# Where a split weight begins in SBUF: moving the up-product weights of a float32 decoder trunk by 32 bytes

## The chip, the cores and the metric

The kernel runs on one core of a Trainium2 chip. A core has a matrix engine (TensorE; PE in the profile, its weight loads PEld), a vector engine (DVE), an activation engine (ACT), GpSimd (POOL) and a queue engine (SP) that issues transfers. All of them work on one on-chip memory, SBUF, which has 128 partitions; a tile is the same range of bytes in every partition. Products are written to a second memory, PSUM. The metric is the device time of one execution in microseconds (us), the median of three runs.

## The reference

The reference is a trunk of four residual blocks on 512 tokens with a model width of 1024, all in float32: multi-head latent attention, a multi-layer perceptron (MLP), gated linear attention, and a second MLP, with an RMS norm ahead of each and one at the end. The MLP is where most of the arithmetic lies:

```python
def sq_relu_mlp(xn, w_up, w_down):            # w_up 1024 x 4096, w_down 4096 x 1024
    hid = jnp.square(jax.nn.relu(xn @ w_up))
    return hid @ w_down
...
x = x + sq_relu_mlp(rms_norm(x, norm_mlp[i]), mlp_w_up[i], mlp_w_down[i])
```

## The kernel before, in words

**Split products.** The matrix engine is used in a float32 mode (`float32r`) that keeps only part of the mantissa, so each operand is split into a high part and the rest. ACT rounds the source into the high part (L104), DVE subtracts to get the low part (L107), and a product is three matrix multiplications: high times high, high times low, low times high. The split weights are called `wh` and `wl`. `piece` (L137) makes such a pair; each of the two tags has three buffers, which all weights of the program use in turn.

A matrix multiplication has a stationary operand, which a weight load (LDWEIGHTS) brings into the array, and a moving operand, which streams through it. Every multiplication here has a weight load of its own, and the load for the next one runs while the current one streams.

**The MLP.** `mlp` runs each layer as a first block of hidden columns (`up_first`, L846) and then seven steps (`step`, L951), one for each further block of 512 hidden columns. Within a step both the up and the down product are cut into quadrants and done with seven quadrant products in place of eight (Strassen's scheme in Winograd's form). So a step has seven up products (`up_product`, L931) and seven down products (`down_product`, L941), which alternate on the matrix engine:

- An up product takes 512 x 256 weights. It has 24 multiplications of 128 x 128 stationary weights (slices of `wh` and `wl`) with 256 moving columns (L939). The moving operand is a split quadrant of the normed activations. Three of the seven quadrants ("11", "21", "22") are halves of tiles of the norm, made by `both_parts` (L96) and called `set` in the profile; the other four are sums of quadrants in tiles of their own, `T1` to `T4` (`quadrants`, L864; the profile calls them all T).
- A down product takes 256 x 512 weights. It has 12 multiplications with 512 moving columns (L948); here the split weights are the moving operand and the split hidden activations, also called `set`, are stationary.

Two layers of seven steps make 14 steps. The weights of the next block come in while a block is computed (`fetch`, L913): SP issues the plain transfers into `comb` and `wraw`, and POOL issues transfers that add to what SP's brought (L918 and L928, four in a step). POOL's transfers are written as lists of descriptors into a scratch region at the bottom of SBUF, 16,384 bytes of each partition.

**What sets the order.** The kernel is written in a tile language with a scheduler: the order of the work follows the order in which the code allocates and issues, with the buffers' reuse as the bound. Tiles get their addresses from the pools, in the order in which their tags first appear. In both programs the order of the instructions on all five engines is the same, row for row; only addresses and line numbers differ. (Two weight tiles, `w_kr` and `wa`, go by the names `wh` and `wl` afterwards.)

**Where the tiles lie.** Start of an operand in its partition, as a remainder of 512 bytes (slices within a tile begin at multiples of 512 bytes, so the remainder is the same for all slices of one tile):

| operand | used as | before | after |
|---|---|---|---|
| `wh`, `wl` in up products | stationary | 32 | 0 |
| `wh`, `wl` everywhere else | stationary or moving | 32 | 32 |
| `set` (norm quadrants, hidden activations, attention outputs) | both | 32 | 32 |
| `T1` to `T4` | moving | 320 | 288 |
| `comb`, two of six buffers (made after the T tiles) | source of splits | 320 | 288 |
| `comb`, the other four | source of splits | 320 | 320 |
| `cq`, the split query latents of attention | moving | 128 | 128 |
| `ckv`, its split key and value latents | moving | 192 | 192 |
| `ADh`, `ADl` in the linear attention (L1515) | stationary | 320 | 320 |

"Distance" below is the moving operand's remainder less the stationary operand's, again as a remainder of 512.

Of the kernel before, what the change touches and what calls it, by code (L numbers as in the profile page):

```python
# [10 lines left out]
F32 = mybir.dt.float32  # L11
F32R = mybir.dt.float32r
# [6 lines left out]
P = 128  # L19
# [3 lines left out]
ND = D // P  # L23
# [5 lines left out]
ROPE = 64  # L29
# [6 lines left out]
RANK = 16  # L36
# [14 lines left out]
def trunk_kernel(ctx: ExitStack, tc: tile.TileContext, t_in: dict, out: bass.AP):  # L51
    nc = tc.nc
# [3 lines left out]
    sb = ctx.enter_context(tc.tile_pool(name="sb", bufs=1))  # L56
    count = [0]

    def uname(s):
        count[0] += 1  # L60
        return f"{s}_{count[0]}"
# [14 lines left out]
    def bank(tag):  # L76
        return psum["pool"].tile([P, 512], F32, tag=f"ps_{tag}", bufs=psum["banks"][tag], name=uname("ps"))
# [11 lines left out]
    def tmp(shape=(P, 512), dt=F32):  # L89
        return sb.tile(list(shape), dt, tag="tmp", bufs=6, name=uname("tmp"))  # L90
# [11 lines left out]
    def split(src, hi, lo, hi_eng=ACT, lo_eng=DVE, order=lambda i: i):  # L102
        if hi_eng is ACT:
            order(ACT.activation(hi, src, AF.Copy))  # L104
        else:
            hi_eng.tensor_copy(hi, src)
        lo_eng.tensor_tensor(lo, src, f(hi), ALU.subtract)  # L107
# [26 lines left out]
        SP.dma_start(raw, src)  # L134
        return raw

    def piece(raw, a, n, order=lambda i: i):  # L137
        hi = sb.tile([P, a, n], F32R, tag="wh", bufs=3, name=uname("wh"))
        lo = sb.tile([P, a, n], F32R, tag="wl", bufs=3, name=uname("wl"))
        split(raw, hi, lo, order=order)  # L140
        return hi, lo

    def cut(pair, *idx):
        return tuple(t[idx] for t in pair)
# [56 lines left out]
    def gcol(name, j):  # L201
        c = GAIN_COL[name] + j
        return gains[:, c : c + 1]
# [166 lines left out]
    def col_chunk(w2d, c0, n):  # L370
        return load(w2d[:, c0 : c0 + n].rearrange("(k p) n -> p k n", p=P), w2d.shape[0] // P, n)


    def mla(layer, nrm, first, pools):
# [36 lines left out]
        KH = ND // 2  # L411
        raw = sb.tile([P, ND, 256], F32, tag="wraw", bufs=2, name=uname("wraw"))
        wq = []
        for h in range(2):
            ks = slice(h * KH, (h + 1) * KH)
            SP.dma_start(raw[:, ks], w_in[:, :256].rearrange("(k p) n -> p k n", p=P)[:, ks])
            wq.append(piece(raw[:, ks], KH, 256))
        for j in range(2):
            p = bank("c")
# [10 lines left out]

        raw = col_chunk(w_in, 256, P)
        w = piece(raw, ND, P)
        p = bank("b")
        a_type(p, w, X)
# [2 lines left out]


        raw = col_chunk(w_in, QL + KL, ROPE)
        wr = sb.tile([P, ND, 2, ROPE], F32R, tag="wh", bufs=3, name="w_kr")  # L440
        ACT.activation(wr[:, :, 1, :], raw, AF.Copy)
        DVE.tensor_tensor(wr[:, :, 0, :], raw, f(wr[:, :, 1, :]), ALU.subtract)
        p = bank("b")
# [23 lines left out]
        raw = sb.tile([P, 2, MH, VD], F32, tag="wraw", bufs=2, name="wraw_v")  # L467
        for k in range(2):
            SP.dma_start(raw[:, k], w_ukv[:, k, :, NOPE:])
        wv = [piece(raw[:, k : k + 1].rearrange("p a h c -> p a (h c)"), 1, D) for k in range(2)]  # L470
        V = [[None, None] for _ in range(NT)]
        VP = []
# [13 lines left out]
        for t in range(NT):  # L486
            tk = slice(t * P, (t + 1) * P)
            for hf in range(2):
                p = bank("bc"[hf])
# [15 lines left out]
            if t == 1:  # L505
# [3 lines left out]
                for j in range(2):  # L509
                    y = tmp()  # L510
                    DVE.scalar_tensor_tensor(y, pkv[j], gcol("kvn", 2 * layer + j), r_kv, ALU.mult, ALU.mult)
                    hi, lo = (keep.tile([P, S], F32R, tag=f"ckv{j}{x}", name=f"ckv{j}{x}") for x in "hl")
# [16 lines left out]
        raw = sb.tile([P, 3, MH, ROPE], F32, tag="wraw", bufs=2, name="wraw_qr")  # L529
# [5 lines left out]
        wa = piece(raw3[:, 0:2], 2, 512)  # L535
        wq = [cut(wa, slice(None), 0), cut(wa, slice(None), 1), wb]
        qs = []
        for t in range(NT):
            tk = slice(t * P, (t + 1) * P)
            p = bank("b")  # L540
# [70 lines left out]
        p = bank("c")[:ROPE]  # L611
# [187 lines left out]
    def mlp(layer, nrm, nxt=None):  # L799
# [3 lines left out]
        KH = ND // 2  # L803
        first, second = slice(0, TH), slice(TH, S)
        es = ExitStack()
        fast = es.enter_context(tc.tile_pool(name=f"fast{layer}", bufs=1, reuse_waits="tile"))
# [11 lines left out]
        def comb(i):  # L818
            return fast.tile([P, 2 * S], F32, tag=f"comb{i}", bufs=1, name=uname("comb"))

        def by_k(t, n):
            return t.rearrange("p (k n) -> p k n", k=n)
# [4 lines left out]
        def signed(src, hi, lo, sign):  # L827
            ACT.activation(hi, src, AF.Copy, scale=sign)
            DVE.scalar_tensor_tensor(lo, src, sign, f(hi), ALU.mult, ALU.subtract)
# [34 lines left out]
        def quadrants():  # L864
            lead, trail = range(KH), range(KH, ND)
            quad["11"] = [nrm.parts[k][:, :, first] for k in lead]
            quad["21"] = [nrm.parts[k][:, :, first] for k in trail]
            quad["22"] = [nrm.parts[k][:, :, second] for k in trail]
            t1, t2, t3, t4 = (by_k(comb(i), KH) for i in range(2, 6))
            for k in lead:  # L870
                g1, g2 = (gcol(nrm.g, nrm.g0 + j) for j in (k, k + KH))
                u, v = xT[k], xT[k + KH]
                ACT.activation(t3[:, k], u[:, second], AF.Copy, scale=g1)
                DVE.scalar_tensor_tensor(t3[:, k], v[:, second], g2, t3[:, k], ALU.mult, ALU.subtract)
                DVE.scalar_tensor_tensor(t2[:, k], u[:, first], g1, t3[:, k], ALU.mult, ALU.add)
                DVE.scalar_tensor_tensor(t4[:, k], v[:, first], g2, t2[:, k], ALU.mult, ALU.subtract)
                DVE.scalar_tensor_tensor(t1[:, k], v[:, second], g2, t2[:, k], ALU.mult, ALU.subtract)
            for name, t, sign in (("T2", t2, -1.0), ("T3", t3, 1.0), ("T1", t1, -1.0), ("T4", t4, -1.0)):
                parts = fast.tile([P, KH, 2, TH], F32R, tag=name, name=uname(name))
                signed(t, parts[:, :, 0], parts[:, :, 1], sign)  # L880
                quad[name] = [parts[:, k] for k in lead]
# [47 lines left out]
            return first_part  # L929

        def up_product(t, a, q, start):  # L931
            w = piece(a, KH, 256)
            for j in range(2):
                o = t[:, j * TH : (j + 1) * TH]
                for k in range(KH):
                    wh, wl = cut(w, slice(None), k, slice(j * P, (j + 1) * P))
                    xh, xl = quad[q][k][:, 0], quad[q][k][:, 1]
                    for n, (a_, x_) in enumerate(((wh, xh), (wh, xl), (wl, xh))):
                        PE.matmul(o, a_, x_, start=start and j == 0 and k == 0 and n == 0, stop=k == KH - 1 and n == 2, skip_group_check=True)  # L939
# [11 lines left out]
        def step(b, q, r, after):  # L951
# [24 lines left out]

            z = bank("u")
            up_product(z, a11, "11", True)
            y = bank("u")
            ACT.activation(y, z, AF.Copy)  # L980
# [5 lines left out]
            e = two_banks("e") if opening else begun(d)  # L986

            up_product(y, a12, "21", False)
            finish(y, 0, 0, r)
            DVE.tensor_tensor(a11, s1, a11, ALU.add)  # L990
# [5 lines left out]
            DVE.tensor_tensor(q11, q11, q12, ALU.add)  # L996

            up_product(z, a11, "T2", False)
            u = tmp()
            ACT.activation(u, z, AF.Copy)  # L1000
# [45 lines left out]

        up_first(Q[0])
        quadrants()
        if not nxt:
            residual()  # L1050
# [58 lines left out]
        if nxt:  # L1109
# [6 lines left out]
            for c in range(2):  # L1116
# [10 lines left out]
                for j, p in enumerate(ps_):  # L1127
                    if j % 2 == 0:
                        w = piece(last_raw[c][:, :, j * P : (j + 2) * P], 4, 256)
                    for k in range(4):  # L1130
                        wh, wl = cut(w, slice(None), k, slice(j % 2 * P, (j % 2 + 1) * P))
# [65 lines left out]
    def gla(layer, nrm, vtag, ytag):  # L1197
# [90 lines left out]
        raw = tmp((P, ND, RANK))  # L1288
        ACT.dma_start(raw, w_in[:, 2 * DK + 2 * D :].rearrange("(k p) n -> p k n", p=P))
        R2 = 2 * RANK  # L1290
        wa = sb.tile([P, ND, 3, 2, RANK], F32R, tag="wl", bufs=3, name="wa")
        raw3 = raw.unsqueeze(2).to_broadcast([P, ND, 3, RANK])
        ACT.activation(wa[:, :, :, 1, :], raw3, AF.Copy)
        DVE.tensor_tensor(wa[:, :, :, 0, :], raw3, f(wa[:, :, :, 1, :]), ALU.subtract)
# [6 lines left out]
        p = bank("a")  # L1301
# [352 lines left out]
    for k0, k1 in ((0, 1), (1, 2), (2, 4), (4, 6), (6, 8)):  # L1654
        w = piece(raw0[:, k0:k1], k1 - k0, KL, tc.keep_in_program_order)
# [7 lines left out]
    turns = rope_turns()  # L1663

    O, begun = mla(0, nrm, w0, mla_pools)
    rope_es.close()
    n_mlp0 = Norm(ND, inv_dr, "mlp", 0)
# [19 lines left out]
    mlp(0, n_mlp0, n_mix1)  # L1687
    psum_layout(False)
    Y, begun = gla(0, n_mix1, "B", "B")
    n_mlp1 = Norm(ND, inv_dr, "mlp", ND)  # L1690
    out_proj(t_in["gla_w_o"][0], Y, n_mlp1, begun)
# [52 lines left out]
```

## Time and profile before

| | |
|---|---|
| median of 3 runs | 1057.3 us (1056.95 to 1057.44) |
| the profiled execution | 1057.37 us |
| its span, first to last instruction | 1055.6 us |
| TensorE busy | 1045.5 us, 99% |
| VectorE busy | 876.0 us, 83% |
| ScalarE busy | 698.6 us, 66% |
| GpSimd busy | 113.4 us, 11% |
| one step of the MLP (steady) | 39.05 us |

The span leaves 1.8 us of the execution outside it. A row of the profile that groups instructions gives the line, the engine, the operation, out<-in by tile names, the shape, the count, the busy time in us and the mean duration of one in ns. Matrix multiplications are pipelined: the duration of one is longer than the distance from its start to the next one's, and it is the latter that adds up to the time. The chain of waits follows the work that ended last back through what released it; its rows give a start, a length and the instructions of that piece.

### The profile page before, as it was taken

The page shows a single profiled execution, that of the slowest core. Times are in us where ns is not written, and L with a number is a line of the kernel's source. Part 1 is how long each engine was busy: PE and PEld are TensorE (multiplying, and loading weights), DVE is VectorE, ACT ScalarE, POOL GpSimd, SP SyncE. Part 2 cuts the span into 40 slices and gives each one's busy share as a digit, 9 for nine tenths or more (in the row PEclk, how much of TensorE's full clock was granted, in tenths as well). Part 3 has the DMA queues.
Part 4 walks back from the last instruction along what each step waited for, and adds up shares of the span by engine and source line. Part 5 has one row for each costly group of instructions (what it writes and reads, how often), then busy time and mean ns, then how long its engine had stood idle before and what let it go on. Part 6 is the DMA issues. An engine that isn't in the chain of part 4 may idle for free.

```text
span 1055.6 us, 15598 instructions
## 1 busy us (share of the span) xinstructions
PE 1045.5 (99%) x5966; PEld 913.7 (87%) x5966; DVE 876.0 (83%) x1340; ACT 698.6 (66%) x1074; POOL 113.4 (11%) x128
## 2 busy tenths in 40 slices
PE   9999999999999999999999999999999999999997
PEld 7888888889999999998888888878889999999985
DVE  7899977979889889898686498469889989989993
ACT  7667664577777767766445565655667777777784
POOL 7410011201101111000000000000011010010000
PEclk9999999999999999999999999999999999999999
DMA  7311235866966976842322221444496696696622
GB/s 231 90 51 41 81 79 160 238 176 150 235 181 150 229 192 146 221 147 93 90 80 80 80 80 51 126 105 132 110 248 132 178 254 140 176 249 152 165 81 80
DMA packets 120493, 149.97 MB, mean 142 GB/s; under 512 B 9345, under 2 KB 86145, under 8 KB 120289
## 3 DMA queue, kind: packets, MB, share of 16 engines
q1 hardware_dynamic: 95920, 117.76, 34.4%
q0 software_dynamic: 22400, 29.36, 17.4%
q10 hardware_dynamic: 2096, 1.84, 0.6%
q8 instruction: 47, 0.77, 0.3%
q14 instruction: 30, 0.24, 0.1%
HBM read 144.49 MB, written 4.19 MB: 141 GB/s over the span
## 4 chain that ended last, share of the span: by engine, by line
PE 95%; ACT 2%; DVE 2%; issue 0%; DMA 0%; ACTq 0%; SPq 0%; DVEq 0%
PE ps L939 26%; PE ps L948 25%; PE ps L112 10%; PE ps L114 10%; PE ps L113 10%; PE ps L1133 2%; PE ps L1388 2%; PE ps L129 1%; PE ps L1168 1%; PE ps L408 1%; PE ps L1515 1%; DVE wl L107 0%; PE ps L671 0%; PE ps L1438 0%; PE ps L667 0%
## 5 line engine op out<-in xcount | busy, mean ns | idle before, releaser
L948 PE MATMUL ps<-wh,set 128*128 128x512 f32 x784 | 258.5, 390 | 0.0
L107 DVE TENSOR_TENSOR wl<-wraw,wh 128x1024 fp32r<-128x1024 f32 x139 | 169.4, 1221 | 39.7 <-ACT wh L104 39.4
L104 ACT ACTIVATE wh<-wraw 128x1024 fp32r<-128x1024 f32 x139 | 145.9, 1053 | 82.1 <-PE ps L113 38.3
L948 PEld LDWEIGHTS ps<-wh,set 128*128 128x128 f32 x784 | 147.3, 188 | 28.8
L104 ACT ACTIVATE wh<-comb 128x1024 fp32r<-128x1024 f32 x112 | 118.8, 1061 | 62.8 <-PE ps L939 41.9
L939 PE MATMUL ps<-T,wh 128*128 128x256 f32 x896 | 159.8, 279 | 0.0
L948 PE MATMUL ps<-wl,set 128*128 128x512 f32 x392 | 153.7, 392 | 0.0
L107 DVE TENSOR_TENSOR wl<-comb,wh 128x1024 fp32r<-128x1024 f32 x112 | 136.7, 1220 | 18.6 <-ACT wh L104 16.9
L939 PEld LDWEIGHTS ps<-T,wh 128*128 128x128 f32 x896 | 140.5, 188 | 4.5
L939 PE MATMUL ps<-T,wl 128*128 128x256 f32 x448 | 125.1, 279 | 1.0 <-DVE wl L107 1.0
L939 PE MATMUL ps<-set,wh 128*128 128x256 f32 x672 | 122.6, 283 | 0.0
L939 PEld LDWEIGHTS ps<-set,wh 128*128 128x128 f32 x672 | 107.4, 191 | 3.2
L112 PE MATMUL ps<-set,wh 128*128 128x512 f32 x280 | 109.3, 392 | 0.7 <-ACT set L1557 0.3
L113 PE MATMUL ps<-set,wh 128*128 128x512 f32 x280 | 109.4, 391 | 0.0
L114 PE MATMUL ps<-set,wl 128*128 128x512 f32 x280 | 109.0, 390 | 0.0
L939 PE MATMUL ps<-set,wl 128*128 128x256 f32 x336 | 95.2, 283 | 0.0
L939 PEld LDWEIGHTS ps<-T,wl 128*128 128x128 f32 x448 | 84.2, 188 | 1.5 <-DVE wl L107 1.4
L948 PEld LDWEIGHTS ps<-wl,set 128*128 128x128 f32 x392 | 73.8, 188 | 11.6
L928 POOL DMA_DIRECT2D comb<-in_mlp_w_down_dram x28 | 33.6, 1201 | 421.0 <-DMA comb<-in_mlp_w_down_dram 155.5
L939 PEld LDWEIGHTS ps<-set,wl 128*128 128x128 f32 x336 | 64.3, 191 | 0.0
L112 PEld LDWEIGHTS ps<-set,wh 128*128 128x128 f32 x280 | 52.5, 188 | 12.6 <-ACT wh L104 1.0
L114 PEld LDWEIGHTS ps<-set,wl 128*128 128x128 f32 x280 | 52.6, 188 | 11.2 <-DVE wl L107 0.4
(396 smaller groups left out, 2024.2 us busy)
## 6 DMA issues: line engine op xcount, KB each, us to landing
comb<-in_mlp_w_down_dram SPq DMA_DIRECT2D x74, 512.0 KB, 5.0
wraw<-in_mlp_w_up_dram SPq DMA_DIRECT2D x32, 1024.0 KB, 5.8
comb<-in_mlp_w_down_dram POOLq DMA_DIRECT2D x28, 512.0 KB, 7.7
wraw<-in_gla_w_in_dram SPq DMA_DIRECT2D x12, 1024.0 KB, 5.3
comb<-in_mlp_w_up_dram SPq DMA_DIRECT2D x14, 512.0 KB, 3.8
comb<-in_mlp_w_up_dram POOLq DMA_DIRECT2D x14, 512.0 KB, 8.4
wraw<-in_mlp_w_up_dram POOLq DMA_DIRECT2D x14, 512.0 KB, 7.2
wraw<-in_mla_w_o_dram SPq DMA_DIRECT2D x4, 1024.0 KB, 5.0
```

The costliest lines, as they stand in the source:

```text
L104: order(ACT.activation(hi, src, AF.Copy))
L107: lo_eng.tensor_tensor(lo, src, f(hi), ALU.subtract)
L112: PE.matmul(psum, wh, xh, start=start, stop=False)
L113: PE.matmul(psum, wh, xl, start=False, stop=False)
L114: PE.matmul(psum, wl, xh, start=False, stop=stop)
L129: PE.transpose(psum, src, ident[: src.shape[0], : src.shape[0]])
L408: PE.matmul(p, w[:, i, j * P : (j + 1) * P], x, start=start, stop=stop)
L928: POOL.dma_start(t, q(b, *more), accum_op=ALU.add)
L939: PE.matmul(o, a_, x_, start=start and j == 0 and k == 0 and n == 0, stop=k == KH - 1 and n == 2, skip_group_check=True)
L948: PE.matmul(o, x_, w_, start=start and k == 0 and n == 0, stop=k == 1 and n == 2, skip_group_check=True)
L1133: PE.matmul(p, a, x, start=False, stop=k == 3 and n == 2, skip_group_check=True)
L1388: PE.matmul(p[:, t - t0], k[:, t * P : (t + 1) * P], moving[:, t], start=True, stop=True)
```

## The change

The shared buffers of the split weights grow from 1024 to 1152 float32 elements. A split weight no longer begins at the start of its buffer but 128 elements (512 bytes) in; the split weights of the up products begin 120 elements (480 bytes) in, so 32 bytes lower than all other pieces. A tile of 120 elements that nothing uses (`gap`) is placed ahead of the T tiles in the MLP's pool, so that these begin 32 bytes lower too, as a remainder of 512. To make room, the scratch region of POOL's transfers is cut from 16,384 to 4,096 bytes of each partition; all tiles behind it move down with it by multiples of 512 bytes. No instruction is added, removed or moved.

```diff
-    def piece(raw, a, n, order=lambda i: i):
-        hi = sb.tile([P, a, n], F32R, tag="wh", bufs=3, name=uname("wh"))
-        lo = sb.tile([P, a, n], F32R, tag="wl", bufs=3, name=uname("wl"))
+    W_ROOM, W_AT, W_AT_UP = 1152, 128, 120
+
+    def room_for(tag, a, n, at=W_AT):
+        t = sb.tile([P, W_ROOM], F32R, tag=tag, bufs=3, name=uname(tag))
+        return t[:, at : at + a * n].rearrange("p (a n) -> p a n", a=a)
+
+    def piece(raw, a, n, order=lambda i: i, at=W_AT):
+        hi = room_for("wh", a, n, at)
+        lo = room_for("wl", a, n, at)
         split(raw, hi, lo, order=order)
         return hi, lo
...
-        wr = sb.tile([P, ND, 2, ROPE], F32R, tag="wh", bufs=3, name="w_kr")
+        wr = room_for("wh", ND, 2 * ROPE).rearrange("p k (a b) -> p k a b", a=2)
...
+            fast.tile([P, 120], F32, tag="gap", name=uname("gap"))
             for name, t, sign in (("T2", t2, -1.0), ("T3", t3, 1.0), ("T1", t1, -1.0), ("T4", t4, -1.0)):
                 parts = fast.tile([P, KH, 2, TH], F32R, tag=name, name=uname(name))
...
         def up_product(t, a, q, start):
-            w = piece(a, KH, 256)
+            w = piece(a, KH, 256, at=W_AT_UP)
...
-        wa = sb.tile([P, ND, 3, 2, RANK], F32R, tag="wl", bufs=3, name="wa")
+        wa = room_for("wl", ND, 6 * RANK).rearrange("p k (r a b) -> p k r a b", r=3, a=2)
...
-    nc = _bacc.Bacc("TRN2", target_bir_lowering=False, num_devices=1)
+    nc = _bacc.Bacc("TRN2", target_bir_lowering=False, num_devices=1, dynamic_dma_scratch_size=4096)
```

## The prediction, made before the changed kernel was run

> **What bounds the kernel now.** I read the page first: its busy times, its slices with the granted clock, and the chain of waits.
>
> ```profile
> span 1055.6 us, 15598 instructions
> PE 1045.5 (99%) x5966; PEld 913.7 (87%) x5966; DVE 876.0 (83%) x1340; ACT 698.6 (66%) x1074; POOL 113.4 (11%) x128
> PEclk9999999999999999999999999999999999999999
> PE 95%; ACT 2%; DVE 2%; issue 0%; DMA 0%; ACTq 0%; SPq 0%; DVEq 0%
> PE ps L939 26%; PE ps L948 25%; PE ps L112 10%; PE ps L114 10%; PE ps L113 10%; PE ps L1133 2%; PE ps L1388 2%; PE ps L129 1%; PE ps L1168 1%; PE ps L408 1%; PE ps L1515 1%; DVE wl L107 0%; PE ps L671 0%; PE ps L1438 0%; PE ps L667 0%
> ```
>
> The matrix engine bounds it: 95% of the chain is its work, at full clock. L939, the up products that the change touches, is the largest part. A busy PE can still be waiting inside, so I next ask who PE waits for in the seven steps of the first MLP, and for the busy times of one step.
>
> ```profile
> PE ps L939 <- DVE wl L107: 0.5, 1, 0.5
> 284.67:323.72 39.05, 39.05 (x255) 35.61 (x254) 34.90 (x39) 28.39 (x36) 4.97 (x4) 1.00 0.74 188
> ```
>
> One wait of 0.5 us in 275 us: nothing but the pace of the multiplications sets a step's 39.05 us. DVE with 34.90 us has 4 us of slack in it, ACT (28.39) ten. A nanosecond off each multiplication comes straight off the time. The chain through the same step shows the paces:
>
> ```profile
> 284.67 2.87 PE ps L939 x24
> 287.55 2.75 PE ps L948 x12
> 290.29 2.87 PE ps L939 x24
> 293.17 2.75 PE ps L948 x12
> 295.91 2.80 PE ps L939 x24
> 298.71 2.75 PE ps L948 x12
> ```
>
> Two up products of the same 24 multiplications take 2.87 us, a third 2.80. PE in order of time tells which (start, length, then what; x2 is two merged):
>
> ```profile
> 284.86 0.40 PE L939 MATMUL ps<-set,wh 128*128 128x256 f32 x2
> ...
> 285.58 0.28 PE L939 MATMUL ps<-set,wh 128*128 128x256 f32 x1
> ...
> 295.75 0.40 PE L939 MATMUL ps<-T,wh 128*128 128x256 f32 x2
> ...
> 296.45 0.39 PE L939 MATMUL ps<-T,wh 128*128 128x256 f32 x2
> ```
>
> Six multiplications lie between each pair of starts: 0.72 / 6 = 120.0 ns apiece with the `set` tile moving, 0.70 / 6 = 116.7 with T. Same shape, same weights, same data type; what differs is where the moving tile lies against the weights: `set` at distance 0 (both begin at 32), T at distance 288 (320 against 32). The groups confirm it over the whole run, for the weight loads too:
>
> ```profile
> L939 PE MATMUL ps<-T,wh 128*128 128x256 f32 x896 | 159.8, 279 | 0.0
> L939 PE MATMUL ps<-T,wl 128*128 128x256 f32 x448 | 125.1, 279 | 1.0 <-DVE wl L107 1.0
> L939 PE MATMUL ps<-set,wh 128*128 128x256 f32 x672 | 122.6, 283 | 0.0
> L939 PE MATMUL ps<-set,wl 128*128 128x256 f32 x336 | 95.2, 283 | 0.0
> L939 PEld LDWEIGHTS ps<-T,wh 128*128 128x128 f32 x896 | 140.5, 188 | 4.5
> L939 PEld LDWEIGHTS ps<-set,wh 128*128 128x128 f32 x672 | 107.4, 191 | 3.2
> ```
>
> Both the stream (283 against 279) and the weight load beside it (191 against 188) are longer at distance 0. My reading is that load and stream, which run at the same time, get in each other's way in SBUF when they walk through the same remainders.
>
> **The change, part by part.**
>
> *Weights of up products at 0 in place of 32.* For `set` products the distance goes from 0 to 32, a value that no row of before has. The counts are 672 + 336 = 1008 multiplications, 42 products (3 in each of 14 steps). I bound the pace by the nearest rows. On the good side stands T, with the same line, shape and neighbours: 2.80 for 2.87 us a product, so 42 x 0.07 = 2.9 us off. Other distances occur in the two attention blocks:
>
> ```profile
> 601.02 0.40 PE L1515 MATMUL ps<-set,ADh 128*128 128x256 f32 x2
> ...
> 602.44 1.23 PE L1515 MATMUL ps<-S,qd 128*128 128x256 f32 x9
> ...
> 590.58 0.39 PE L113 MATMUL ps<-set,wh 128*128 128x512 f32 x1
> ...
> 592.39 0.39 PE L112 MATMUL ps<-set,wh 128*128 128x512 f32 x1
> ...
> 70.47 0.40 PE L113 MATMUL ps<-cq0l,wh 128*128 128x512 f32 x1
> ...
> 72.58 0.39 PE L113 MATMUL ps<-ckv0l,wh 128*128 128x512 f32 x1
> ```
>
> Twelve multiplications of 256 columns at distance 224 start between 601.02 and 602.44: 118.3 ns apiece, between T and `set`. With 512 columns it is the other way round: at distance 0 eight take 1.81 us, 226.3 ns apiece; at 96 and 160 nine take 2.11 us, 234.4. So a distance other than 0 helped wherever 256 columns move and hurt where 512 do. Up products move 256, and T is the row that shares all but the distance; I take its pace for `set`: **-2.9 us**. The bounds are, above, 1008 x 8.1 = 8.2 us slower, by the 512-column rows, and, below T, the 113 ns that would be left if a pace of 120 lost twice what T gains: 1008 x 6.7 = 6.8 us faster.
>
> *T tiles at 288 in place of 320.* Their distance stays 288. 1344 multiplications. If the distance alone counts, nothing moves: I take 0. If the tile's own remainder counts, T would lose what sets it apart from `set`: 56 x 0.07 = 3.9 us slower at worst.
>
> *All other pieces* keep 32 against 32 or their old distance, because the whole of SBUF behind the scratch moves by multiples of 512 bytes: 0. The joints between products change (the last of a down product now streams while a weight at 0 loads, two joints for each of 98 up products); the chain shows 2.75 us for a down product after either kind of up product, so I put the joints at 0, with 98 x 0.01 = 1 us either way as bound.
>
> *The splits that write these weights.* ACT's and DVE's outputs move by 32 bytes, and two `comb` buffers with them.
>
> ```profile
> L104 ACT ACTIVATE wh<-wraw 128x1024 fp32r<-128x1024 f32 x139 | 145.9, 1053 | 82.1 <-PE ps L113 38.3 <-PE ps L114 19.1 <-issue 9.7
> L104 ACT ACTIVATE wh<-comb 128x1024 fp32r<-128x1024 f32 x112 | 118.8, 1061 | 62.8 <-PE ps L939 41.9 <-PE ps L948 6.0 <-issue 4.9
> ```
>
> The two sources, which begin at different remainders, differ by 8 ns. Even on all 98 up products that is 0.8 us, spread over an engine with ten us of slack a step: 0. Were that cover gone, 0.8 us.
>
> *The smaller scratch.* POOL might wait for room, or lists might be written later. A transfer's time to landing and its first reader, for the tightest of the four in a step, which brings the sum that DVE adds at the next step's start:
>
> ```profile
> 264.53 1.30 POOL L928 DMA_DIRECT2D comb<-in_mlp_w_up_dram  x1 [2.46 <-DMA comb<-in_mlp_w_up_dram]
> 285.01 1.22 DVE L990 TENSOR_TENSOR wraw<-comb,wraw 128x1024 f32<-128x1024 f32 x1
> comb<-in_mlp_w_up_dram POOLq DMA_DIRECT2D x14, 512.0 KB, 8.4
> ```
>
> Issued at 264.5 and landed 8.4 us later, it is read 12 us after that. So a delay costs nothing until it passes 12 us: 0.
>
> Sum: -2.9 us on the profiled execution's 1057.37 us, 1054.4 us; that execution lies 0.1 us above the median, so the same holds for the runs.
>
> **A rule weighed against the rows.** The Trainium skill, "TensorE: Matmul & The Clock Gate", section "Step-by-step: what each phase is for", says that the engine has two independent SBUF read ports, so that loading the next weights takes no read bandwidth from the running multiplication. By that rule the distance could not matter. No run here separates the two readings, and the rows above that bear on it differ in both the distance and the moving tile's own place.
>
> **The rivals.**
>
> *The moving tile's own place counts, not the distance.* `set`, at 32 beyond a multiple of 64, then stays at 2.87 us, and the T tiles, which go from a multiple of 64 to 32 beyond one, slow from 2.80 to 2.87: 56 x 0.07 = +3.9, 1061.3 us. For it: T and `set` differ in just this. Against it: `ADh` rows have a moving tile at 32 and run at 118.3, not 120. I give it 0.10. (It is what the port rule of the Trainium skill, named above, would leave as an explanation.) In a weaker form the place counts for neither, the gap has another cause and the change does nothing: 1057.4 us, 0.05.
>
> *Half the gain.* Away from 0 and 288 a 256-column stream may run at the 118.3 ns of the `ADh` rows. `set` (2.87 / 24 = 119.6) gains 1.3 ns x 1008 = 1.3 us, 1056.1 us; if T too, in its new place, ran so, it would lose 1.6 x 1344 = 2.2 us and the net is +0.8, 1058.2 us. For it: two of the three 256-column paces lie at or above 118. Against: that stream is short, 12 in a row, and T's is the longer. 0.20 together.
>
> *A worse distance* (the other side). At 32 the load and the stream may never fall into step, as in the 512-column rows at 96 and 160, which run 8.1 ns above distance 0. The place is the 1008 `set` multiplications; the price is 8.2 us at full size, 1065.6 us, and half that if it goes by columns, 1061.5 us. It decides from 2.1 ns on. For it: distance 32 is untried and closer to 0 than any other. Against: no 256-column row is slower than distance 0. 0.13.
>
> *The scratch is too small* and POOL's transfers come more than 12 us late, DVE's sum with them, and PE waits in each step: for 13 us, 14 x 1 = 14 us. Nothing in the rows speaks for it; POOL is busy 4.97 us of a step. 0.02.
>
> *More than T's pace*, with both operands' new places, down to 113 ns: around 1051 us, 0.05.
>
> **How the numbers follow.** The forecast, `set` at T's pace, has 0.45; its own range is 1053.6 to 1055.1 (the joints' 1 us and the reading of 0.07). Two tenths of a percent, 2.1 us, is about what a measurement of this kernel tells from no change. Faster than 1055.2: the forecast and the better case, 0.50. Within: half the gain and no effect, 0.25. Slower: 0.10 + 0.13 + 0.02 = 0.25. The range of 1053.0 to 1061.5 holds the forecast, half the gain, no effect, the moving tile's place and a part of the worse distance, some 0.83.
>
> **What would show it.** In the profile after, the chain should show `set` products at 2.80 us, the L939 rows with `set` at 279 ns and their weight loads at 188, T unchanged at 2.80, L948 unchanged at 2.75. It is wrong if T products read 2.87 (the moving tile's place), if `set` reads 2.84 (half) or above 2.90 (worse distance), or if the waits of PE name DVE or a transfer in the steps (scratch).

## The result and the profile after

The changed kernel takes 1054.92 us (median; 1054.59 to 1055.96), the kernel before, run beside it, 1057.12 us. The ratio is 0.9978, with an interval of 0.9971 to 0.9985: 1.6 to 3.1 us faster, 2.2 us by the medians. The forecast was 1054.4 us.

The profiled execution took 1055.56 us, 0.6 us more than the median; the steps of its first MLP begin 0.7 us later than those of before (at 206.49 us for 205.77). The change is not what delays them: in e2 below, which leaves out only the gap tile, they begin at 205.71. The head of its page:

```profile
span 1053.8 us, 15598 instructions
PE 1043.6 (99%) x5966; PEld 911.0 (86%) x5966; DVE 876.8 (83%) x1340; ACT 699.4 (66%) x1074; POOL 111.7 (11%) x128
```

The busy times in the step that the prediction showed (start and end, the length, then PE, PEld, DVE, ACT and POOL with their counts, the clock, the DMA share, GB/s):

```profile
285.07:323.94 38.87, 38.87 (x255) 35.38 (x254) 34.88 (x39) 28.48 (x36) 4.99 (x4) 1.00 0.75 189
```

And the only wait of the up products for another engine in the first MLP:

```profile
PE ps L946 <- DVE wl L107: 0.6, 1, 0.6
```

The same 15,598 instructions, the same full clock, and PE as busy as the step is long: it is the pace of the multiplications that changed. A step takes 38.87 us in place of 39.05, and 14 x 0.18 = 2.5 us. The chain of waits shows where (L946 is now the line of the up products, L955 that of the down products; start, length, piece):

```profile
285.07 2.80 PE ps L946 x24
287.88 2.75 PE ps L955 x12
290.63 2.80 PE ps L946 x24
293.43 2.75 PE ps L955 x12
296.18 2.80 PE ps L946 x24
298.98 2.75 PE ps L955 x12
```

The first and the third row are `set` products, 2.80 us where 2.87 stood; the fifth is a T product, 2.80 as before. The groups of instructions say the same for the whole run (first the down products' row of before, then rows of after):

```profile
L948 PE MATMUL ps<-wh,set 128*128 128x512 f32 x784 | 258.5, 390 | 0.0
```

```profile
L955 PE MATMUL ps<-wh,set 128*128 128x512 f32 x784 | 259.3, 391 | 0.0
L946 PE MATMUL ps<-T,wh 128*128 128x256 f32 x896 | 159.7, 279 | 0.0
L946 PE MATMUL ps<-set,wh 128*128 128x256 f32 x672 | 119.7, 280 | 0.0
L946 PEld LDWEIGHTS ps<-set,wh 128*128 128x128 f32 x672 | 105.2, 188 | 3.5
L946 PE MATMUL ps<-set,wl 128*128 128x256 f32 x336 | 93.8, 279 | 0.0
```

`set` rows fell from 283 to 279 and 280 ns, the weight loads beside them from 191 to 188. One row rose: the down products, from 258.5 us before to 259.3. To see how much a whole product took, I measured from the start of its first multiplication to the start of the next product's first, and took the mean over products whose records are complete:

| product | count in the run | before, us | after, us | difference x count, us |
|---|---|---|---|---|
| up, `set` | 42 | 2.872 | 2.799 | -3.1 |
| up, T | 56 | 2.8025 | 2.798 | -0.2 |
| down | 98 | 2.744 after T, 2.7475 after `set` | 2.755 | +0.9 |
| sum | | | | -2.4 |

Most of the rise of the down products sits in their last multiplication. This is the order of time at one such joint, first before (L948, L939), then after:

```profile
289.90 0.39 PE L948 MATMUL ps<-wh,set 128*128 128x512 f32 x1
290.13 0.40 PE L939 MATMUL ps<-set,wh 128*128 128x256 f32 x2
```

```profile
290.23 0.40 PE L955 MATMUL ps<-wh,set 128*128 128x512 f32 x1
290.47 0.40 PE L946 MATMUL ps<-set,wh 128*128 128x256 f32 x2
```

From the start of the last down multiplication to that of the next product lie 0.23 us before and 0.24 after; the mean over all joints is 226 ns and 235 ns. In that moment the down product's `wh`, at 32, streams while the first weights of the next up product, now at 0, are loaded: the distance at the joint went from 0 to 32, and with 512 columns that cost 8 ns.

### The profile page after: what moved, and what is told of

It is laid out like the page before. It is cut to its first block, busy times and chain, and to the rows that moved or that the text cites. A ratio compares the mean times of both kernels' runs of the same rounds, so it can differ in the third digit from the quotient of the medians.

```text
span 1053.8 us, 15598 instructions
## 1 busy us (share of the span) xinstructions
PE 1043.6 (99%) x5966; PEld 911.0 (86%) x5966; DVE 876.8 (83%) x1340; ACT 699.4 (66%) x1074; POOL 111.7 (11%) x128
## 4 chain that ended last, share of the span: by engine, by line
PE 95%; ACT 2%; DVE 2%; issue 0%; DMA 0%; ACTq 0%; SPq 0%; DVEq 0%
PE ps L955 26%; PE ps L946 26%; PE ps L112 10%; PE ps L114 10%; PE ps L113 10%; PE ps L1140 2%; PE ps L1395 2%; PE ps L129 1%; PE ps L1175 1%; PE ps L414 1%; PE ps L1522 1%; DVE wl L107 0%; PE ps L1445 0%; PE ps L677 0%; PE ps L673 0%
## 5 line engine op out<-in xcount | busy, mean ns | idle before, releaser
L955 PE MATMUL ps<-wh,set 128*128 128x512 f32 x784 | 259.3, 391 | 0.0
L955 PEld LDWEIGHTS ps<-wh,set 128*128 128x128 f32 x784 | 147.1, 188 | 28.8
L946 PE MATMUL ps<-T,wh 128*128 128x256 f32 x896 | 159.7, 279 | 0.0
L955 PE MATMUL ps<-wl,set 128*128 128x512 f32 x392 | 153.7, 392 | 0.0
L946 PEld LDWEIGHTS ps<-T,wh 128*128 128x128 f32 x896 | 140.4, 188 | 4.9
L946 PE MATMUL ps<-T,wl 128*128 128x256 f32 x448 | 125.1, 279 | 1.2 <-DVE wl L107 1.2
L946 PE MATMUL ps<-set,wh 128*128 128x256 f32 x672 | 119.7, 280 | 0.0
L946 PEld LDWEIGHTS ps<-set,wh 128*128 128x128 f32 x672 | 105.2, 188 | 3.5
L946 PE MATMUL ps<-set,wl 128*128 128x256 f32 x336 | 93.8, 279 | 0.0
L946 PEld LDWEIGHTS ps<-T,wl 128*128 128x128 f32 x448 | 84.2, 188 | 1.7 <-DVE wl L107 1.6
L955 PEld LDWEIGHTS ps<-wl,set 128*128 128x128 f32 x392 | 73.6, 188 | 11.6
L112 PEld LDWEIGHTS ps<-set,wh 128*128 128x128 f32 x280 | 52.5, 188 | 12.6 <-ACT wh L104 1.0
L946 PEld LDWEIGHTS ps<-set,wl 128*128 128x128 f32 x336 | 63.2, 188 | 0.0
```

Of the source, the lines that this page charges most:

```text
L112: PE.matmul(psum, wh, xh, start=start, stop=False)
L955: PE.matmul(o, x_, w_, start=start and k == 0 and n == 0, stop=k == 1 and n == 2, skip_group_check=True)
```

## The experiments

All are edits of the changed kernel. "Distance" is the moving operand's place less the stationary one's, as a remainder of 512 bytes, as in the table of places above. Product times are those of the method just told; chain rows are from the same step of the first MLP as above, and the line numbers of up and down products differ by a line or two. The theory: a distance of 0 costs a 256-column stream time. The main rival: the place of one operand alone counts. Summary first, each told below:

| run | places: `set` / T against up weights | time, us | before, us | ratio, interval | `set`, T, down product, us |
|---|---|---|---|---|---|
| before | 32 / 320 against 32 | | 1057.12 | | 2.872, 2.803, 2.744 to 2.748 |
| after | 32 / 288 against 0 | 1054.92 | 1057.12 | 0.9978 (0.9971 to 0.9985) | 2.799, 2.798, 2.755 |
| e1_room_only | 32 / 320 against 32 | 1057.31 | 1057.12 | 1.000 (0.9991 to 1.001) | 2.872, 2.803, 2.744 to 2.748 |
| e2_no_gap | 32 / 320 against 0 | 1052.72 | 1057.12 | 0.996 (0.9946 to 0.9974) | 2.799, 2.723, 2.755 to 2.790 |
| e3_up_64_lower | 32 / 256 against 480 | 1054.21 | 1057.12 | 0.9974 (0.9963 to 0.9985) | 2.824, 2.806, 2.728 to 2.731 |
| e4_both_32_lower | 0 / 288 against 0 | 1061.66 | 1057.12 | 1.0043 (1.0028 to 1.0058) | 2.875, 2.798, 2.738 to 2.755 |
| e5_up_at_320 | 32 / 32 against 224 | 1054.78 | 1057.35 | 0.9976 (0.9967 to 0.9986) | 2.824, 2.824, 2.731 |
| e6_down_at_320 | 32 / 320 against 0 | 1057.37 | 1057.35 | 1.0001 (0.9992 to 1.001) | 2.802, 2.824, 2.764 |
| e7_up_at_256 | 32 / 32 against 288 | 1060.88 | 1057.35 | 1.0033 (1.0019 to 1.0047) | 2.873, 2.873, 2.748 |
| e8_all_64 | 64 / 320 against 0 | 1051.86 | 1057.09 | 0.9949 (0.9934 to 0.9964) | 2.726, 2.723, 2.789 |
| e9_all_64_other_side | 0 / 256 against 64 | 1059.99 | 1057.09 | 1.0027 (1.0017 to 1.0038) | 2.827, 2.828, 2.778 |

### Room and scratch alone

```diff
-    W_ROOM, W_AT, W_AT_UP = 1152, 128, 120
+    W_ROOM, W_AT, W_AT_UP = 1152, 128, 128
...
-            fast.tile([P, 120], F32, tag="gap", name=uname("gap"))
```

> The changed kernel with the up-product weights back at 32 (distance 0 to the norm's tiles) and without the gap tile: only the larger weight buffers and the smaller scratch of POOL's transfers remain. Both theories (the distance between the loaded weights and the moving tile counts; the weights' own place counts) expect the old paces: 2.87 us an up product with set, 2.80 with T, and no lengthening at the end of a down product; 1057.1 us within 0.2%. If the gain came from the room or the scratch instead, this run shows 1054.9 us.

The larger buffers and the smaller scratch stay, every distance is that of before. Time and product times are those of before too, to the nanosecond in the table. The chain, first a `set` product and then a T product:

```profile
284.64 2.87 PE ps L945 x24
...
295.88 2.80 PE ps L945 x24
```

So the room, the addresses moved by multiples of 512 bytes and the smaller scratch cost nothing that this measurement can tell. What the change does, it does by the 32 bytes.

### Weights and `set` both lower

```diff
-        return sb.tile([P, 2, S], F32R, tag="set_A", bufs=8, name=uname("set"))
+        t = sb.tile([P, 2 * S + 128], F32R, tag="set_A", bufs=8, name=uname("set"))
+        return t[:, 120 : 120 + 2 * S].rearrange("p (a s) -> p a s", a=2)
```

> The changed kernel with the norm's split tiles also 32 bytes lower, so that these and the up-product weights both begin at 0: distance 0 again, but both at a multiple of 64. If the distance counts, up products with set go back to 2.87 us; if the weights' own place (or a moving tile at a multiple of 64) counts, they stay at 2.80 us. In the other products the norm's tiles then lie at distance 480 from their weights, with 512 columns moving: if those rows follow the 512-column rows of the attention, they cost up to 8 ns each, some 800 of them, 6.7 us; so the whole time is 1058 us (distance 0 costs, 512 columns unhurt) to 1065 us, or 1055 to 1062 us by the other theory. The pace of the up products decides.

Now the norm's tiles lie at 0 as well as the up weights: the distance is 0 again, in a new place. The chain (`set` first, T after) and the groups:

```profile
285.84 2.88 PE ps L947 x24
...
297.07 2.80 PE ps L947 x24
```

```profile
L947 PE MATMUL ps<-set,wh 128*128 128x256 f32 x672 | 122.7, 283 | 0.0
L114 PE MATMUL ps<-set,wh 128*128 128x512 f32 x280 | 110.3, 395 | 0.0
```

The `set` products fall back to 2.88 us and 283 ns a multiplication, though the weights stayed at 0. That the weights' new place by itself made them faster is refuted. The second row shows why this kernel is slower than before and not equal to it: the norm's tiles serve all four blocks, and in the products of 512 columns ahead of, between and behind the MLPs' steps the distance went from 0 to 480 or 32. Matched one by one with those of e1, 1,003 such multiplications went from a median of 227 ns to one of 234 and take 4.5 us longer together, as much as the medians differ. The steps themselves take as long as before.

### Without the gap

```diff
-            fast.tile([P, 120], F32, tag="gap", name=uname("gap"))
```

> The changed kernel without the gap tile: T tiles stay at 320, the up-product weights lie at 0, so T's distance is 320, a multiple of 64, where it was 288. If the distance counts as a remainder of 512, T keeps about 2.80 us and the time stays at 1054.9 us. If only its remainder of 64 counts, T falls to distance 0 and to 2.87 us: 56 x 0.07 = 3.9 us slower, 1058.8 us. If the weights' own place counts, T keeps 2.80 us, 1054.9 us.

The T tiles stay at 320, so their distance is 320 and not 288. The chain (`set` and the down product behind it, T and its down product):

```profile
284.09 2.80 PE ps L945 x24
286.89 2.75 PE ps L954 x12
...
295.20 2.72 PE ps L945 x24
297.92 2.79 PE ps L954 x12
```

T products fall to 2.72 us, which none of the three expectations had. PE in order of time shows a pace that no row of before had, 0.68 us from one start to the other with six multiplications between them, 113.3 ns apiece:

```profile
295.38 0.39 PE L945 MATMUL ps<-T,wh 128*128 128x256 f32 x2
...
296.06 0.39 PE L945 MATMUL ps<-T,wh 128*128 128x256 f32 x2
```

That is 56 x 0.075 = 4.2 us off. About half comes back in the down products behind T, 2.790 us in place of 2.755: 56 x 0.035 = 2.0 us. Net 2.2 us, which is what lies between 1054.92 and 1052.72. The part of the change that keeps T's distance at 288 costs those 2.2 us. Where the down product loses them is seen in its first, fifth and last multiplications, here of this run and then of the changed kernel, where the T products run at 116.7 ns:

```profile
297.76 0.40 PE L954 MATMUL ps<-wh,set 128*128 128x512 f32 x1
...
298.70 0.40 PE L954 MATMUL ps<-wl,set 128*128 128x512 f32 x1
...
300.32 0.40 PE L954 MATMUL ps<-wh,set 128*128 128x512 f32 x1
```

```profile
298.82 0.40 PE L955 MATMUL ps<-wh,set 128*128 128x512 f32 x1
...
299.75 0.39 PE L955 MATMUL ps<-wl,set 128*128 128x512 f32 x1
...
301.34 0.40 PE L955 MATMUL ps<-wh,set 128*128 128x512 f32 x1
```

The first four multiplications take nearly the same, 0.94 and 0.93 us; the next seven take 1.62 us here and 1.59 in the changed kernel. There they settle at 227 ns after five, here they go on changing between 224 and 236 ns to the end, though their own distance is 0 in both: a product's pace depends for a while on what ran ahead of it.

### Only the weights' place: 256 and 320

The T tiles are brought to 32, where `set` lies, so that both kinds of product must behave alike; the two runs differ in the weights alone.

```diff
# e7_up_at_256 (e5_up_at_320 has W_AT_UP = 48 instead of 64)
-    W_ROOM, W_AT, W_AT_UP = 1152, 128, 120
+    W_ROOM, W_AT, W_AT_UP = 1152, 128, 64
...
-            fast.tile([P, 120], F32, tag="gap", name=uname("gap"))
+            fast.tile([P, 56], F32, tag="gap", name=uname("gap"))
```

> Up-product weights at 224 and a shorter gap, so that both set and T lie at distance 320 from them, which gave T 113.3 ns a multiplication (2.72 us a product) in the run without the gap. All operands here begin 32 beyond a multiple of 64. If the distance alone sets the pace: both at 2.72 us, 42 x 0.074 = 3.1 us less than the run without the gap in the up products, 1049.6 us before what the joints give back. If the pace of 113.3 needed operands at multiples of 64: both stay at 2.80 us or above, 1054.9 us. The joints (how fast the down products settle) may take or give 35 ns each, 98 x 0.035 = 3.4 us.

> Up-product weights at 288, set and T at 32, so both at distance 256, half of 512. If the worst case is distance 0 as a remainder of 512 and the best is far from it, both run at about 2.72 us, 1049.6 us before the joints. If the remainder of 64 counts as well (256 is a multiple of 64, like 0, 64 and 320, of which 0 gave 120.0, 64 gave 117.7 and 320 gave 113.3), it falls between these: 2.72 to 2.87 us a product, 1049.6 to 1058 us.

The chain of e7 (`set`, then T), and that of e5:

```profile
285.23 2.87 PE ps L946 x24
...
296.46 2.87 PE ps L946 x24
```

```profile
284.01 2.82 PE ps L946 x24
...
295.11 2.82 PE ps L946 x24
```

In both, `set` and T take the same time: brought to the same place, the two kinds of product no longer differ. At a distance of 256 both pay what distance 0 pays, 2.87 us; at 320 both take 2.82. Between the two runs no 256-column moving tile moved, only the weights, so the place of the moving tile alone is refuted too. That e5 would come to 2.72 us, as T did at distance 320 in the run without the gap, was wrong: the distance does not decide alone.

### Weights 64 bytes lower

```diff
-    W_ROOM, W_AT, W_AT_UP = 1152, 128, 120
+    W_ROOM, W_AT, W_AT_UP = 1152, 128, 112
...
-            fast.tile([P, 120], F32, tag="gap", name=uname("gap"))
+            fast.tile([P, 112], F32, tag="gap", name=uname("gap"))
```

> Up-product weights 64 bytes below the others in place of 32 (at 480, so again 32 beyond a multiple of 64), gap shortened so that T's distance stays 288. Distance to set is 64. If the distance counts as a remainder of 512: set at 2.80 us, 1054.9 us. If it counts as a remainder of 64, or if the weights' own place at a multiple of 64 made the gain: set back at 2.87 us, 42 x 0.07 = 2.9 us slower than the changed kernel, 1057.8 us.

The chain: a `set` product and the down product behind it, then a T product.

```profile
284.15 2.82 PE ps L946 x24
286.98 2.73 PE ps L955 x12
...
295.26 2.81 PE ps L946 x24
```

At distance 64 `set` takes 2.82 us, 117.7 ns a multiplication, between the two values expected: twice the shift brings 0.048 us a product where 32 bytes brought 0.073. T, still at 288, keeps 2.81. The down products drop from 2.755 to 2.73 us. Of these 26 ns, 9 are the joint into the next up product, which is back at 226 ns (its distance is 64); the rest is that their first multiplications settle at 227 ns sooner. That gives 98 x 0.026 = 2.5 us, and pays for the slower `set` (42 x 0.025 = 1.1 us) and T products (56 x 0.008 = 0.4 us): 1.0 us net against the changed kernel, of which the medians show 0.7.

### The down products at distance 320

```diff
-            fast.tile([P, 120], F32, tag="gap", name=uname("gap"))
...
-            wh, wl = piece(a, 2, 512)
+            wh, wl = piece(a, 2, 512, at=80)
```

> The run without the gap, and the weights of the down products (moving, 512 columns) at 352, so at distance 320 from the stationary tile at 32, in place of 0. If distance 320 helps 512 columns as it helped 256 (6.7 ns less each): 14 x 7 x 12 = 1176 x 6.7 = 7.9 us faster than the run without the gap, 1044.9 us. If 512 columns run at 234 ns at every distance but 0, as all rows so far: 1176 x 8 = 9.4 us slower, 1062 us.

This is the kernel without the gap, with the moving operand of the down products at 352 in place of 32. The chain, a T product and the down product behind it:

```profile
295.88 2.83 PE ps L945 x24
298.71 2.77 PE ps L954 x12
```

The down multiplications take 230 ns each and never settle at 226.7: between the two expectations, and no gain for 512 columns. More telling is what I did not expect: the T products, whose operands lie where they lay without the gap, lose the 113.3 ns and take 2.824 us, 117.7 apiece. So at one and the same distance, with every operand of the product in the same place, there are two paces. What differs is the place of the down products' weights: those that stream ahead of a T product, and those that ACT and DVE write while it runs. This run doesn't tell which of the two matters.

### All up products at 64 mod 128

```diff
# e8_all_64 (no gap; the norm's tiles for the MLP at 64, up weights at 0)
-    W_ROOM, W_AT, W_AT_UP = 1152, 128, 120
+    W_ROOM, W_AT, W_AT_UP = 1152, 0, 120
...
-            parts = self.parts[j] = both_parts()
+            parts = self.parts[j] = both_parts(8 if self.g == "mlp" else 0)
```

```diff
# e9_all_64_other_side (the norm's tiles for the MLP at 0, up weights at 64, T at 256)
-    W_ROOM, W_AT, W_AT_UP = 1152, 128, 120
+    W_ROOM, W_AT, W_AT_UP = 1152, 0, 8
...
-            parts = self.parts[j] = both_parts()
+            parts = self.parts[j] = both_parts(120 if self.g == "mlp" else 0)
...
-            fast.tile([P, 120], F32, tag="gap", name=uname("gap"))
+            fast.tile([P, 112], F32, tag="gap", name=uname("gap"))
```

In both, `W_AT` of 0 leaves all other weights at 32, `both_parts` takes its tiles 128 elements larger and hands out a part of them, and the weights of the MLP's first block are placed like the norm's tiles.

> No gap, up-product weights at 0, and the MLP norm's split tiles at 64 (with the first block's weights, which meet them with 512 columns, at 64 too): set at distance 64, T at 320, the joint from a down product into an up product at distance 32 as in the run without the gap. If distance 64 has two paces, 113.3 and 117.7, and the way in from the down product picks one, set now takes T's fast one: 2.72 us a product with the down product after it at 2.79 us, so a pair of 5.51 us where set had 5.55 us: 42 x 0.04 = 1.7 us less than without the gap, 1051.0 us. If the pace of 113.3 belongs to 320 alone (as a remainder of 512), set stays at 2.80 to 2.82 us: 1052.7 to 1053.8 us.

> As the run before in this call, but from the other side: up-product weights at 64, set at 0 (distance 448) and T at 256 (distance 192), so all 64 beyond a multiple of 128; the joint into an up product is at distance 480 and the one out of it at 480 or 224, where it was 32 or 288. If only the remainder of 128 counts for the pace and the way in picks 113.3 or 117.7: 2.72 or 2.82 us for set and T alike. With 2.72 and down products that settle early (2.73 us, as with weights at 480) a pair is 5.45 us, 98 x 0.06 = 5.9 us under the first run of this call; with 2.82 and 2.73, 5.55 us, 98 x 0.04 = 3.9 us over it.

The chain of e8 (`set` and its down product, T and its down product), the busy times of its step, and the chain of e9:

```profile
284.43 2.73 PE ps L946 x24
287.15 2.79 PE ps L955 x12
...
295.45 2.73 PE ps L946 x24
298.18 2.79 PE ps L955 x12
```

```profile
284.43:323.00 38.57, 38.57 (x254) 34.84 (x254) 34.78 (x39) 28.50 (x35) 4.99 (x4) 1.00 0.76 193
```

```profile
284.62 2.83 PE ps L947 x24
287.45 2.78 PE ps L956 x12
```

e8 has all but three of its up products at 113.3 ns, at two distances (64 for `set`, 320 for T), and with 1051.86 us it beats both kernels. At 2.723 us each they would save 7.4 us against the changed kernel (42 x 0.076 + 56 x 0.075); 98 x 0.034 = 3.3 us of it go back into the down products. That leaves 4.1 us, or 14 x 0.30 us by the step shown. The steps of both MLPs together are 3.6 us shorter in the traces, in part because the first products of a layer are slower; the medians show 3.1. e9 has distances of 448 and 192, which are 64 beyond a multiple of 128 as well, and sits at 117.8 ns in its steady steps. Its down products take 2.78 us and not the expected 2.73, so it is 2.9 us slower than before. It differs from e8 in the joint ahead: the down product's last stream, at 32, lies 32 from the weights being loaded in e8, and 480 in e9.

In steady steps, 113.3 ns came only at distances of 64 beyond a multiple of 128, and only where the joint's distance was 32 (e2's T, e8); where it was 64 (e3), 320 (e5), 352 (e6) or 480 (e9), the same kind of distance gave 117.7 or 117.8. With down weights at 32, as in all runs but e6, a joint of 32 is the same as up weights at 0, so these runs can't tell the two apart. And neither decides alone, as the first products of a layer show, which begin after other work or after a wait. In e2 the first T product of each layer runs at 117.8 ns, and so do three products of e8: the first `set` product of each layer and the first T product of the second. In e9 it is the other way round. This is its first T product, at distance 192; PE waits 0.55 us in it for split weights:

```profile
214.59 0.38 PE L947 MATMUL ps<-T,wl 128*128 128x256 f32 x1 [0.55 <-DVE wl L108]
...
215.17 0.39 PE L947 MATMUL ps<-T,wh 128*128 128x256 f32 x2
...
216.19 0.39 PE L947 MATMUL ps<-T,wh 128*128 128x256 f32 x2
```

Nine multiplications lie between the last two starts, 1.02 / 9 = 113.3 ns apiece. So within one run, with every operand at the same remainders of 512, both paces occur: at 320 in e2 and e8, at 192 in e9. How a product starts takes part in the choice. What selects the pace isn't shown, and a kernel that has up products of 2.72 us together with down products of 2.73 wasn't tried.

## Why the prediction was right, and where it was not

**The pace of `set` products** (put at T's pace, -2.9 us): right. They went to 2.799 us, -3.1 us over 42 products, and the weight loads to 188 ns as named. The reason given, the distance between load and stream, holds against both of its rivals: with the weights still at 0 and distance 0 restored, the 2.88 us returned, and with the moving tiles fixed at 32, moving only the weights took the same products from 2.82 to 2.87. What these runs show is that the relative place counts; that load and stream meet in SBUF, as the prediction reads it, is not shown. That 32 gives just the pace of 288 was luck: the prediction took it from T as the nearest row, with none at 32, and at 64 the same reasoning would have met 42 x 0.048 = 2.0 us in e3.

**The moving tile's own place** (rival, 1061.3 us): wrong in its place and in its price; T tiles moved by 32 bytes at the same distance kept 2.80 us. The port rule that the prediction names with it, from the Trainium skill ("TensorE: Matmul & The Clock Gate", "Step-by-step: what each phase is for"), that loading takes no read bandwidth from the running multiplication, would by itself leave the place of the weights without effect; in e5 and e7 that place set the pace at 117.7 or 120.0 ns. Whether read bandwidth is what the two contend for, these runs don't show.

**T tiles** (put at 0): right for this change, 2.8025 to 2.798 us. What the step did not see is that the place they had left would have been worth 2.2 us more with the new weights, at distance 320: the nearest rows then gave 113 ns only as an extreme, with a chance of 0.05.

**The joints** (put at 0, bound 1 us either way): this term was mis-sized. It measured +0.9 us, nearly all of its bound. The step read 2.75 us "after either kind of up product" from the chain, but in before the joint out of a down product had distance 0 ahead of either kind, so those rows could not tell what a joint at 32 costs. The prediction's own 512-column rows, slower by 8.1 ns away from distance 0, would have: a joint is one multiplication of 512 columns, 98 x 8.1 ns = 0.8 us, with the sign known. (Not every other distance is slow there: at 64 and 320, in e3 and e5, the joint stayed at 226 ns.)

**Splits and scratch** (put at 0): right. The run with room and scratch alone has the time of before. The tightest of POOL's transfers, its issue and its first reader in the order of time, and then the median time to landing, of the changed kernel:

```profile
265.26 1.30 POOL L935 DMA_DIRECT2D comb<-in_mlp_w_up_dram  x1 [2.58 <-DMA comb<-in_mlp_w_up_dram]
...
285.40 1.22 DVE L997 TENSOR_TENSOR wraw<-comb,wraw 128x1024 f32<-128x1024 f32 x1
```

```profile
comb<-in_mlp_w_up_dram POOLq DMA_DIRECT2D x14, 512.0 KB, 9.2
```

The median time to landing is 9.2 us in place of 8.4, and the tile is read 20 us after the issue: the slack of 12 us became 11.

**The sum**: -2.9 forecast; -3.1 - 0.2 + 0.9 = -2.4 by the products, -2.2 by the medians. Of the rivals, the worse distance and half the gain did not happen at 32 bytes; a weaker gain was met 64 bytes lower (2.824 us in e3).

## What to carry to other kernels

Where every multiplication has its own weight load and the matrix engine is the bound, the start of the moving and of the stationary tile against each other, in steps of 32 bytes, is a size to measure: here it was worth up to 5.6 per cent of a 256-column multiplication (120.0 to 113.3 ns), without one more instruction. A start that suits one shape can cost another: of the distances tried here, 0 was the best for whole products of 512 columns and, with 256, the worst for products of 256 columns, so each use gets a buffer place of its own. When a place is moved, cost the joints too, since the last stream of one product runs beside the first load of the next, at a distance of its own.

## What was not expected of the hardware

- The paces of 256-column multiplications go by the distance as a remainder of 128, as far as it was tried: 120.0 ns at 0 and 256; a mean of 116.6 to 116.7 at 32 and 288, in the changed kernel by turns between 113 and 120; 117.7 or 117.8 at 64, 192, 320 and 448, and at times 113.3 at 64, 192 and 320. The twelve at 224 that the prediction shows took 118.3.
- The same operands at the same addresses ran at 113.3 ns in e2 and at 117.7 in e6, for as long as a product lasts; only the down products' weights lay elsewhere. In e9 one T product ran at 113.3 ns where the others ran at 117.8. A pace read from one product is thus not a property of its addresses alone.
- The time of a down product at distance 0 goes with what ran ahead of it and with its joint: 2.73 us in e3 and e5, 2.755 in the changed kernel, 2.79 behind the 113.3 ns products of e2 and e8. It isn't the pace ahead alone, for in e9 it is 2.78 behind 117.8 ns, and in e3 and e5 2.73 behind 117.7. Part of a gain in one product can be paid in the next.
